# VectorE in the order of emission, column sums that yield to mixing steps, and 16 transposes fewer, in a two-layer hybrid mixer on one core

## The chip, the cores and the metric

The kernel runs on one core of a Trainium2 chip. The metric is the device time of one execution in microseconds (us), as the median of several runs; lower is better.

## What is computed

Two layers, each one pre-norm mixer with adaptive modulation; 256 latent tokens and 256 context tokens of width 2048, all in f32. The reference, cut to what matters:

```python
proj = h @ w_in                      # h: modulated RMSNorm of the tokens
q, k, v = heads(proj...)             # 8 heads of 128; q and k with 2-D rope (latent tokens)
y_f = (fourier_mix(f_x) * silu(f_g)) @ w_up_fourier
y_p = (pool_mix(p_x) * silu(p_g)) @ w_up_pool
o_f, s_f = retention_scan(q, k, v, log_gamma[0], s0_fwd)
o_b, s_b = retention_scan(flip(q), flip(k), flip(v), log_gamma[1], s0_bwd)
y_r = (head_rms(o_f + o_b) * silu(r_g)) @ w_up_ret
g = sigmoid(gate_logits)             # three merge gates of width 2048
out = (g_0 * y_f + g_1 * y_p + g_2 * y_r) @ w_out
x = x + gate * out                   # gate, shift, scale come from silu(c) @ w_ada
```

Only the latent tokens come out. In the last layer the context tokens are therefore needed for the retention state alone (their k and v).

## The kernel before

**Weights as a stream.** Every large product is made of three products in a rounded f32 format: hi·hi, lo·hi and hi·lo, where a value is split into a rounded part (hi) and its remainder (lo). `mm3` (L149) issues the three on TensorE (L151 to L153). The weights pass as *chunks* of two k-tiles (128 rows each) by up to 512 columns; some 520 of them, here numbered from 0. `stream` (L243) goes through them; in iteration i it

- prepares chunk i+2: ScalarE writes `whi` (L206), VectorE subtracts to get `wlo` (L207), three buffers each;
- starts the load of chunk i+4 on SyncE's queue (L196, `raw`, four buffers);
- issues the products of chunk i, 24 matmuls of 128x512 where there are four token tiles or column groups ("four units"), 12 where there are two;
- may run one *background unit* (below).

**Mixing steps.** What lies between the large products (rope, head transposes, retention states, scores, head norms, Fourier and pooling steps, splits) is put into a queue as small steps (`Steps`, `mix.append(fn, gap, after)`). After each unit of a chunk, `products` calls `mix.passed(us)`, which issues the steps that are due: `after` is the time in us from its entry, `gap` the time until the next step may follow. So a step's matmuls get their place between the units' matmuls when the program is built. The steps that matter here: `rope_a` (two GpSimd products, L597, per tile), `rope_b` (VectorE, L604 and L605), `heads_T` (four TensorE transposes per head, L684, and a ScalarE copy, L686), `decayed` (L692), `decays_a` (L708, L709), `scores` (L732, L734), `norm_b` (a VectorE reciprocal L766 and a product L767), `gated` (product L614, then a split of the result: hi on ScalarE L431, lo on VectorE L432).

**Background units.** The modulation needs silu(c) @ w_ada for the second layer, computed as column sums on VectorE: 512 KB of w_ada are loaded (`bgraw`, two buffers), then four scalar_tensor_tensor on 128x512 follow (L468; the first of a sum is L466), or two for units of one vector. They are queued in `bg`.

**What sets the order.** TensorE runs in the order in which the program emits its instructions, from the first streamed block to the end: the whole kernel is under `manual_schedule` with TensorE alone. VectorE, ScalarE, GpSimd and SyncE run in an order of the framework's scheduler, which places each engine's instructions by its own estimate of when their inputs are ready.

**Chunk numbers used below** (layer 0, four units, about 5.45 us each): K of head half 0: 0 to 7, Q: 8 to 15, V, K and Q of half 1: 16 to 39, retention gates to 55, merge gates and up-projections from 56 to 215, output projection 216 to 255 (from 240 on two units). Last layer: q 256 to 263, v, k, q, v, k to 303, retention gates 304 to 319, merge gates and up-projections 320 to 479, output projection to the end (mostly two units, 2.72 us). The mixing of a block runs while the next ones stream. At the end of the output projection the residual is added (L1011, L1012), ScalarE sums squares (L1017) and takes a root (L1021), VectorE reduces and inverts (L1020, L1022) and prepares a row scale (L1077).

```python
        for i in range(n):
            prepare(i + 2)
            ahead(i + 4)
            chunks[i][0].products(chunks[i][1], parts.pop(i))
            if i > 5 and i % 8 in (1, 3, 5, 6, 7) and bg:
                bg.popleft()()
```

Of the kernel before, what the change touches and what calls it, by code (L numbers as in the profile page):

```python
# [19 lines left out]
P = 128  # L20
# [4 lines left out]
SEQ = 256  # L25
# [18 lines left out]
def hybrid_kernel(ctx: ExitStack, tc: tile.TileContext, a: dict, out: bass.AP):  # L44
# [15 lines left out]
    def acc():  # L60
        return accp.tile([P, 512], F32, tag="acc", name=nm("acc"))

    def mx():
        return mxp.tile([P, 512], F32, tag="mx", name=nm("mx"))
# [95 lines left out]
    bg = deque()  # L160
# [21 lines left out]
    mix = Steps()  # L182
# [58 lines left out]
    def stream(blocks):  # L241
        chunks = [(b, k0) for b in blocks for k0 in range(0, b.nkt, 2)]
        n = len(chunks)  # L243
        raws, parts = {}, {}

        def ahead(i):
            if i < n:
                raws[i] = chunks[i][0].load(chunks[i][1])

        def prepare(i):  # L250
            if i < n:
                parts[i] = chunks[i][0].split(chunks[i][1], raws.pop(i))

        for i in range(4):
            ahead(i)
        for i in range(2):
            prepare(i)
        yield
        for i in range(n):
            prepare(i + 2)  # L260
            ahead(i + 4)
            chunks[i][0].products(chunks[i][1], parts.pop(i))
            if i > 5 and i % 8 in (1, 3, 5, 6, 7) and bg:
                bg.popleft()()


# [1 line left out]
    with tc.tile_pool(name="start", bufs=1) as sp:  # L268
# [128 lines left out]
        v0_acc = [acc() for _ in range(4)]  # L397
        rg_acc = [acc(), mx(), mx()]
# [126 lines left out]
    def layer(l):  # L525
        last = l == DEPTH - 1
        tok0, ntok = (0, NTOK) if not last else (SEQ, SEQ)
        seqs = (0, 1) if not last else (1,)
        tiles = (0, 1, 2, 3) if not last else (2, 3)
# [45 lines left out]
        def evac(ps):  # L575
            o = g()
            S.copy(o, ps)  # L577
            return o
# [11 lines left out]
        def rope_a(src, t):  # L590
            rope4 = cst["rope"].rearrange("p (t k c) -> p t k c", t=2, k=2)
            o, r2 = src[t], g()
            pv = o.rearrange("p (h f x c) -> p h f x c", h=4, f=2, x=2)
            rv = r2.rearrange("p (h f x c) -> p h f x c", h=4, f=2, x=2)
            sv = rope4[:, t - 2, 1, :].rearrange("p (f x c) -> p f x c", f=2, x=2)
            for x in range(2):
                G.tensor_tensor(rv[:, :, :, x, :], pv[:, :, :, 1 - x, :], sv[:, :, x, :].unsqueeze(1).to_broadcast([P, 4, 2, 32]), op=ALU.mult)  # L597
            rope_r[t] = r2

        def rope_b(src, t):  # L600
            rope4 = cst["rope"].rearrange("p (t k c) -> p t k c", t=2, k=2)
            o = src[t]
            ov = o.rearrange("p (h c) -> p h c", h=4)
            V.tensor_tensor(ov, ov, rope4[:, t - 2, 0, :].unsqueeze(1).to_broadcast([P, 4, P]), op=ALU.mult)  # L604
            V.tensor_tensor(o, o, rope_r.pop(t), op=ALU.add)  # L605
# [16 lines left out]
        class Half:  # L622
# [11 lines left out]
            def k_done(self, t, ps):  # L634
                self.k[t] = evac(ps)
                if t == 3:
                    for t2 in (2, 3):
                        mix.append(lambda t2=t2: rope_a(self.k, t2), gap=0.8, after=2.0)
                    mix.append(lambda: self.decayed(0), gap=1.6)
                    for t2 in (2, 3):  # L640
                        mix.append(lambda t2=t2: rope_b(self.k, t2), gap=1.0)
                    mix.append(lambda: (self.state(0), self.decayed(1)), gap=1.6)
                    for hh in range(4):
                        mix.append(lambda hh=hh: self.heads_T(self.k, (0, 1, 2, 3), self.kT, hh))
                    mix.append(lambda: self.state(1))
                    if last:
                        self.queue_heads()

            def q_done(self, t, ps):
                self.q[t] = evac(ps)  # L650
                if t == 3:
                    for t2 in (2, 3):
                        mix.append(lambda t2=t2: rope_a(self.q, t2), gap=1.2, after=2.0)
                    for t2 in (2, 3):
                        mix.append(lambda t2=t2: rope_b(self.q, t2), gap=1.0)
                    for hh in range(4):
                        mix.append(lambda hh=hh: self.heads_T(self.q, tiles, self.qT, hh))
                    if not last:
                        self.queue_heads()
# [65 lines left out]
            def scores(self, hh):  # L725
                E = self.dec[hh][0]
                for s in seqs:
                    ps = mx()
                    qs = self.qT[hh][:, s * SEQ - tok0:s * SEQ - tok0 + SEQ]
                    for jt in range(2):  # L730
                        k0 = s * SEQ + jt * P
                        T.matmul(ps[:, jt * SEQ:(jt + 1) * SEQ], self.kT[hh][:, k0:k0 + P], qs, start=True, stop=True)  # L732
                    self.at[hh, s] = g()
                    V.scalar_tensor_tensor(self.at[hh, s], ps, QSCALE, E, op0=ALU.mult, op1=ALU.mult)  # L734
# [295 lines left out]
        if last:  # L1030
# [7 lines left out]
            def done(j, t, ps, c0=0, n=512):  # L1038
                xo = projected(j, t, ps, c0, n)
                V.tensor_tensor(xo, xo, fgs[j][:, c0:c0 + n], op=ALU.mult)  # L1040
                xg.setdefault(t, []).append((xo, 512 * j + c0, n))
                if 512 * j + c0 + n == D:
                    for i, (xo, o, n) in enumerate(xg[t]):
                        if i % 2:
                            S.activation(xo, xo, AF.Copy, scale=rs[t])
                        else:
                            V.tensor_scalar(xo, xo, rs[t], None, op0=ALU.mult)
                        nc.sync.dma_start(out=out[0, (t - 2) * P:(t - 1) * P, o:o + n], in_=xo)
# [7 lines left out]
            for c0 in (0, 256):  # L1056
                blocks.append(Block(wview("w_out", l, 512 * 3, 512), KT, 512, [("T", c0, 3 * P - tok0, 256)], flat(m),
                                    lambda u, ps, c0=c0: done(3, 3, ps, c0, 256), keep=kept))
# [67 lines left out]
    blocks0, halves0, rg_done0 = layer(0)  # L1126
    blocks1, _, _ = layer(1)
    for j in range(4):
        bg_mod(1, j)
    run = stream(blocks0 + blocks1)  # L1130
    next(run)
    for t in range(4):
        halves0[0].v_done(t, v0_acc[t])
    for i, ps in enumerate(rg_acc):
        rg_done0(i, ps)
    for _ in run:
        pass


def _constants():  # L1140
# [78 lines left out]
```

## Time and profile before

| what | value |
|---|---|
| median of 3 runs | 2446.63 us (2446.52 to 2446.91) |
| the profiled execution | 2445.55 us, its span 2443.8 us |
| mean granted TensorE clock | 0.995 |
| TensorE busy | 2392.4 us (98%) |
| VectorE / ScalarE / GpSimd busy | 1320.6 (54%) / 870.4 (36%) / 240.3 us (10%) |

The table says that TensorE is busy nearly all of the span; 100% minus its share is what any change of order can win without removing matmuls. Durations of single instructions and places of waits are not in it; they are in the rows further down. Two things help in reading those. A listed matmul lasts 0.39 us, but the next one starts 0.227 us later, because matmuls overlap; the step between starts is the cost. Instructions on VectorE start up to about 0.08 us before the listed end of the one before.

### The profile page before, as it was taken

The page shows a single profiled execution, that of the slowest core. Times are in us where ns is not written, and L with a number is a line of the kernel's source. Part 1 is how long each engine was busy: PE and PEld are TensorE (multiplying, and loading weights), DVE is VectorE, ACT ScalarE, POOL GpSimd, SP SyncE. Part 2 cuts the span into 40 slices and gives each one's busy share as a digit, 9 for nine tenths or more (in the row PEclk, how much of TensorE's full clock was granted, in tenths as well). Part 3 has the DMA queues.
Part 4 walks back from the last instruction along what each step waited for, and adds up shares of the span by engine and source line. Part 5 has one row for each costly group of instructions (what it writes and reads, how often), then busy time and mean ns, then how long its engine had stood idle before and what let it go on. Part 6 is the DMA issues. An engine that isn't in the chain of part 4 may idle for free.

```text
span 2443.8 us, 28705 instructions
## 1 busy us (share of the span) xinstructions
PE 2392.4 (98%) x11288; PEld 1967.8 (81%) x11288; DVE 1320.6 (54%) x1656; ACT 870.4 (36%) x1180; POOL 240.3 (10%) x246
## 2 busy tenths in 40 slices
PE   6999999999999999999999999999999999999998
PEld 3678788778888888888888888878889888888886
DVE  4437657768256258644457432653527544545555
ACT  5222332342222232222222322563426444444444
POOL 0000200200000001110011210230302000110100
PEclk9999999999999999999999999999999999999999
DMA  9955424346345336545466343443335666676664
GB/s 338 348 170 173 138 78 148 92 136 213 115 144 187 93 119 210 156 128 169 130 202 215 112 129 112 147 150 103 100 90 146 211 191 180 181 216 183 189 204 146
DMA packets 226471, 396.58 MB, mean 162 GB/s; under 512 B 14032, under 2 KB 55376, under 8 KB 226336
## 3 DMA queue, kind: packets, MB, share of 16 engines
q1 hardware_dynamic: 221088, 379.74, 50.8%
q0 software_dynamic: 5248, 15.01, 2.1%
q8 instruction: 88, 1.44, 0.2%
q14 instruction: 47, 0.39, 0.1%
HBM read 392.60 MB, written 2.10 MB: 162 GB/s over the span
## 4 chain that ended last, share of the span: by engine, by line
PE 81%; issue 8%; DMA 5%; DVE 4%; POOL 1%; ACT 1%; SPq 0%; DVEq 0%; POOLq 0%; ACTq 0%
PE acc L151 25%; PE acc L152 25%; PE acc L153 25%; DVE bga L468 2%; DMA wa<-in_w_ada_dram 2%; DMA bgraw<-in_w_ada_dram 1%; DVE wlo L207 1%; PE mx L323 1%; PE mx L744 1%; PE mx L732 1%; PE mx L747 1%; POOL g L1085 1%; PE mx L701 0%; DMA raw<-in_w_out_dram 0%; PE mx L889 0%
## 5 line engine op out<-in xcount | busy, mean ns | idle before, releaser
L207 DVE TENSOR_TENSOR wlo<-raw,whi 128x1024 fp32r<-128x1024 f32 (+1 forms) x504 | 624.6, 1240 | 824.5 <-ACT whi L206 824.0
L206 ACT ACTIVATE whi<-raw 128x1024 fp32r<-128x1024 f32 (+1 forms) x504 | 529.2, 1050 | 1153.4 <-PE acc L153 553.5
L151 PE MATMUL acc<-whi,hm 128*128 128x512 f32 x1568 | 621.9, 397 | 0.7 <-ACT g L577 0.7
L152 PE MATMUL acc<-wlo,hm 128*128 128x512 f32 x1568 | 611.7, 390 | 2.2 <-DVE wlo L207 2.2
L153 PE MATMUL acc<-whi,hm 128*128 128x512 f32 x1568 | 611.7, 390 | 0.0
L151 PE MATMUL acc<-hm,whi 128*128 128x512 f32 (+1 forms) x1232 | 461.1, 374 | 0.7 <-ACT whi L206 0.7
L153 PE MATMUL acc<-hm,wlo 128*128 128x512 f32 (+1 forms) x1232 | 453.0, 368 | 1.0 <-DVE wlo L207 1.0
L152 PE MATMUL acc<-hm,whi 128*128 128x512 f32 (+1 forms) x1232 | 452.7, 367 | 0.0
L152 PEld LDWEIGHTS acc<-wlo,hm 128*128 128x128 f32 x1568 | 295.1, 188 | 62.7 <-DVE wlo L207 4.1
L153 PEld LDWEIGHTS acc<-whi,hm 128*128 128x128 f32 x1568 | 294.7, 188 | 62.3
L151 PEld LDWEIGHTS acc<-whi,hm 128*128 128x128 f32 x1568 | 295.0, 188 | 61.2 <-ACT g L577 1.1
L468 DVE SCALAR_TENSOR_TENSOR bga<-bgraw,sc,bga 128x512 f32<-128x512 f32 x420 | 311.8, 789 | 53.1 <-DMA bgraw<-in_w_ada_dram 51.5
L151 PEld LDWEIGHTS acc<-hm,whi 128*128 128x128 f32 x1232 | 232.6, 189 | 42.4 <-ACT whi L206 2.2
L153 PEld LDWEIGHTS acc<-hm,wlo 128*128 128x128 f32 x1232 | 232.4, 189 | 40.5 <-DVE wlo L207 2.2
L152 PEld LDWEIGHTS acc<-hm,whi 128*128 128x128 f32 x1232 | 232.6, 189 | 39.4 <-issue 1.4
L852 POOL TENSOR_TENSOR g<-g,g 128x512 f32<-128x512 f32 x32 | 52.7, 1673 | 726.5 <-DVE g L848 726.5
L151 PE MATMUL acc<-g,whi 128*128 128x512 f32 x256 | 99.7, 390 | 0.0
L152 PE MATMUL acc<-g,whi 128*128 128x512 f32 x256 | 99.6, 389 | 0.0
L153 PE MATMUL acc<-g,wlo 128*128 128x512 f32 x256 | 99.6, 389 | 0.0
L597 POOL TENSOR_TENSOR g<-g,g 128x256 f32<-128x256 f32 x32 | 29.6, 954 | 332.4 <-ACT g L577 332.4
L151 PEld LDWEIGHTS acc<-g,whi 128*128 128x128 f32 x256 | 48.1, 188 | 10.1
L152 PEld LDWEIGHTS acc<-g,whi 128*128 128x128 f32 x256 | 48.1, 188 | 10.0
(213 smaller groups left out, 1888.4 us busy)
## 6 DMA issues: line engine op xcount, KB each, us to landing
raw<-in_w_in_dram SPq DMA_DIRECT2D x368, 512.0 KB, 3.7
bgraw<-in_w_ada_dram SPq DMA_DIRECT2D x128, 512.0 KB, 4.3
raw<-in_w_out_dram SPq DMA_DIRECT2D x72, 512.0 KB, 3.6
wa<-in_w_ada_dram SPq DMA_DIRECT2D x128, 256.0 KB, 6.0
raw<-in_w_up_ret_dram SPq DMA_DIRECT2D x32, 512.0 KB, 3.8
raw<-in_w_up_fourier_dram SPq DMA_DIRECT2D x16, 512.0 KB, 3.7
raw<-in_w_up_pool_dram SPq DMA_DIRECT2D x16, 512.0 KB, 4.4
w<-in_w_in_dram SPq DMA_DIRECT2D x8, 512.0 KB, 6.6
```

What stands on the lines that cost most here:

```text
L151: T.matmul(ps, ah, bh, start=first, stop=False)
L152: T.matmul(ps, ah, bl, start=False, stop=False)
L153: at["product"] = T.matmul(ps, al, bh, start=False, stop=last)
L206: S.activation(hi[:, :, 0:w], raw[:, :, 0:w], AF.Copy)
L207: V.tensor_tensor(lo[:, :, 0:w], raw[:, :, 0:w], hi[:, :, 0:w].bitcast(F32), op=ALU.subtract)
L323: T.matmul(ps[32 * g4:32 * g4 + 32, 0:2 * n * P], sc32[:, kt, :], wa[gi, kt // rows][:, kt % rows, :, :].rearrange("p i c -> p (i c)"), st ...
L468: V.scalar_tensor_tensor(accs[ci, v], raw[:, kk, :], s, accs[ci, v], op0=ALU.mult, op1=ALU.add)
L597: G.tensor_tensor(rv[:, :, :, x, :], pv[:, :, :, 1 - x, :], sv[:, :, x, :].unsqueeze(1).to_broadcast([P, 4, 2, 32]), op=ALU.mult)
L732: T.matmul(ps[:, jt * SEQ:(jt + 1) * SEQ], self.kT[hh][:, k0:k0 + P], qs, start=True, stop=True)
L744: T.matmul(o, self.v[2 * s + jt][:, c], at[:, jt * SEQ:(jt + 1) * SEQ], start=jt == 0, stop=jt == 1 and s == 0)
L747: T.matmul(o, self.st[d][:, c], qd[:, d * SEQ:(d + 1) * SEQ], start=False, stop=d == 1)
L852: G.tensor_tensor(merged[d][:, 0:ntok], merged[d][:, 0:ntok], o[:, 0:ntok], op=ALU.add)
```

## The change

Four edits:

1. From the first streamed block on, VectorE too runs in the order of emission (`manual_schedule` with VectorE around the stream). TensorE did so already; the other engines stay with the scheduler.
2. A background unit is run when fewer than two mixing steps are queued and the chunk's number is no multiple of four, instead of at five fixed chunks of eight.
3. Between the rope steps lies more time: `gap` 0.8 to 1.6 for k, 1.2 to 2.5 for q.
4. In the last layer only the latent tokens' keys are transposed: two transposes per head instead of four (eight heads, so 16 fewer), and `scores` counts its columns from there.

```diff
@@ stream @@
-            if i > 5 and i % 8 in (1, 3, 5, 6, 7) and bg:
+            if i > 5 and len(mix.q) < 2 and i % 4 and bg:
                 bg.popleft()()
@@ Half.k_done @@
-                        mix.append(lambda t2=t2: rope_a(self.k, t2), gap=0.8, after=2.0)
+                        mix.append(lambda t2=t2: rope_a(self.k, t2), gap=1.6, after=2.0)
...
-                        mix.append(lambda hh=hh: self.heads_T(self.k, (0, 1, 2, 3), self.kT, hh))
+                        mix.append(lambda hh=hh: self.heads_T(self.k, tiles, self.kT, hh))
@@ Half.q_done @@
-                        mix.append(lambda t2=t2: rope_a(self.q, t2), gap=1.2, after=2.0)
+                        mix.append(lambda t2=t2: rope_a(self.q, t2), gap=2.5, after=2.0)
@@ scores @@
-                        k0 = s * SEQ + jt * P
+                        k0 = s * SEQ - tok0 + jt * P
@@ end of the program @@
     run = stream(blocks0 + blocks1)
-    next(run)
-    for t in range(4):
-        halves0[0].v_done(t, v0_acc[t])
-    for i, ps in enumerate(rg_acc):
-        rg_done0(i, ps)
-    for _ in run:
-        pass
+    with tc.manual_schedule(engines={mybir.EngineType.DVE}):
+        next(run)
+        for t in range(4):
+            halves0[0].v_done(t, v0_acc[t])
+        for i, ps in enumerate(rg_acc):
+            rg_done0(i, ps)
+        for _ in run:
+            pass
```

`tiles` is (0, 1, 2, 3) in layer 0 and (2, 3) in the last; `tok0` is 0 and 256.

What the order becomes on VectorE is seen in three places. A row gives the line, the operation, and output<-inputs with numbers that differ between the two programs; `bga` is a column sum, `wlo` a chunk's remainder.

**The rope of q, half 0** (chunks 15 to 18). Before, the last of the column sums ahead of it, then the rope:

```order
L468 SCALAR_TENSOR_TENSOR bga_2208<-bgraw_2455,sc,bga_2208 128x512
L468 SCALAR_TENSOR_TENSOR bga_2206<-bgraw_2543,sc,bga_2206 128x512
L468 SCALAR_TENSOR_TENSOR bga_2208<-bgraw_2543,sc,bga_2208 128x512
L604 TENSOR_TENSOR g_1983<-g_1983,g_1379 128x512
L604 TENSOR_TENSOR g_1991<-g_1991,g_1379 128x512
L207 TENSOR_TENSOR wlo_2000<-raw_1923,whi_1999 128x1024
L605 TENSOR_TENSOR g_1983<-g_1983,g_2012 128x512
L605 TENSOR_TENSOR g_1991<-g_1991,g_2022 128x512
```

Now:

```order
L207 TENSOR_TENSOR wlo_1952<-raw_1883,whi_1951 128x1024
L207 TENSOR_TENSOR wlo_1990<-raw_1919,whi_1989 128x1024
L207 TENSOR_TENSOR wlo_2030<-raw_1955,whi_2029 128x1024
L604 TENSOR_TENSOR g_1979<-g_1979,g_1381 128x512
L605 TENSOR_TENSOR g_1979<-g_1979,g_2002 128x512
L604 TENSOR_TENSOR g_1987<-g_1987,g_1381 128x512
L605 TENSOR_TENSOR g_1987<-g_1987,g_2019 128x512
L207 TENSOR_TENSOR wlo_2078<-raw_1993,whi_2077 128x1024
```

The six column sums that stood right ahead of the rope are gone from here; the four rope instructions stand together behind the `wlo` of chunk 19.

**The head norms of half 1** (chunks 55 to 61). Before, one reciprocal between two `wlo` at most:

```order
L766 RECIPROCAL g_3421<-g_3421 128x512
L207 TENSOR_TENSOR wlo_3635<-raw_3603,whi_3634 128x2x128
L207 TENSOR_TENSOR wlo_3651<-raw_3620,whi_3650 128x2x128
L207 TENSOR_TENSOR wlo_3673<-raw_3638,whi_3672 128x2x128
L767 TENSOR_TENSOR g_3420<-g_3420,g_3421 128x512
L766 RECIPROCAL g_3459<-g_3459 128x512
L207 TENSOR_TENSOR wlo_3685<-raw_3654,whi_3684 128x2x128
L207 TENSOR_TENSOR wlo_3707<-raw_3676,whi_3706 128x1024
L767 TENSOR_TENSOR g_3458<-g_3458,g_3459 128x512
L207 TENSOR_TENSOR wlo_3727<-raw_3688,whi_3726 128x1024
```

Now, from the `wlo` of chunk 58 on:

```order
L207 TENSOR_TENSOR wlo_3614<-raw_3587,whi_3613 128x1024
L766 RECIPROCAL g_3346<-g_3346 128x512
L767 TENSOR_TENSOR g_3345<-g_3345,g_3346 128x512
L766 RECIPROCAL g_3390<-g_3390 128x512
L767 TENSOR_TENSOR g_3389<-g_3389,g_3390 128x512
L766 RECIPROCAL g_3447<-g_3447 128x512
L767 TENSOR_TENSOR g_3446<-g_3446,g_3447 128x512
L207 TENSOR_TENSOR wlo_3654<-raw_3603,whi_3653 128x1024
L766 RECIPROCAL g_3486<-g_3486 128x512
L767 TENSOR_TENSOR g_3485<-g_3485,g_3486 128x512
L614 TENSOR_TENSOR g_2406<-g_2406,g_3437 128x512
L432 TENSOR_TENSOR g_3687<-g_2406,g_3686 128x512
```

Three reciprocals with their products now stand between two `wlo`; behind them come pairs of a gate product (L614) and its split (L432), and four column sums before the `wlo` of chunk 61.

**The start of the output projection of layer 0** (chunk 216). The 16 splits of the merged branches, which its products read, stood one or two per `wlo`, from that of chunk 208 to that of chunk 218, before:

```order
L207 TENSOR_TENSOR wlo_9313<-raw_9244,whi_9312 128x1024
L432 TENSOR_TENSOR hm_9643<-g_4013,hm_9642 128x512
L207 TENSOR_TENSOR wlo_9347<-raw_9278,whi_9346 128x1024
L432 TENSOR_TENSOR hm_9647<-g_4021,hm_9646 128x512
L432 TENSOR_TENSOR hm_9651<-g_4029,hm_9650 128x512
L207 TENSOR_TENSOR wlo_9377<-raw_9316,whi_9376 128x1024
```

Now all 16 follow the `wlo` of chunk 218:

```order
L848 TENSOR_TENSOR g_9564<-acc_9593,g_9564 128x512
L207 TENSOR_TENSOR wlo_9639<-raw_9570,whi_9638 128x1024
L432 TENSOR_TENSOR hm_9645<-g_3896,hm_9644 128x512
L432 TENSOR_TENSOR hm_9649<-g_3904,hm_9648 128x512
L432 TENSOR_TENSOR hm_9653<-g_3912,hm_9652 128x512
L432 TENSOR_TENSOR hm_9657<-g_3920,hm_9656 128x512
```

The first ones have moved from eight chunks ahead of their use to the moment of it. In the same way the instructions at the end of the output projection (L1011 to L1022) now stand in one piece per tile between two `wlo`, and the last layer's reciprocals stand two and four together. The column sums of the second layer's output gates, which were done in layer 0 before, now come in the last layer's merge-gate blocks.

## Rows read from the trace of the kernel before

**Rows 1.** Profile page, section 1: busy time of each engine.
```profile
PE 2392.4 (98%) x11288; PEld 1967.8 (81%) x11288; DVE 1320.6 (54%) x1656; ACT 870.4 (36%) x1180; POOL 240.3 (10%) x246
```

**Rows 2.** Waits of TensorE: line <- releaser: us, times, longest.
```profile
PE mx L732 <- DVE g L734: 5.9, 1, 5.9
PE mx L684 <- DVE g L605: 5.0, 3, 4.6
```

**Rows 3.** Stretches: length, busy PE, PEld, DVE, ACT, POOL, granted clock, DMA.
```profile
250.00:262.00 12.00, 7.32 (x31) 5.64 (x30) 12.00 (x17) 1.81 (x3) 2.10 (x2) 0.82 0.62 181
262.00:275.00 13.00, 13.00 (x60) 10.61 (x59) 11.36 (x18) 6.04 (x10) 1.06 (x1) 0.91 0.68 219
440.00:456.00 16.00, 10.10 (x38) 8.02 (x37) 16.00 (x19) 5.39 (x10) 10.63 (x10) 0.79 0.24 64
465.00:530.00 65.00, 63.25 (x277) 51.39 (x276) 38.75 (x43) 27.23 (x40) 5.17 (x6) 1.00 0.39 122
530.00:1560.00 1030.00, 1029.11 (x4597) 848.29 (x4596) 538.22 (x653) 280.57 (x341) 70.30 (x65) 1.00 0.49 150
1560.00:1630.00 70.00, 67.03 (x302) 53.86 (x301) 54.08 (x77) 54.34 (x105) 36.41 (x40) 1.00 0.52 161
```

**Rows 4.** Stretches behind the two longest waits, and one near the end, same columns.
```profile
260.00:262.00 2.00, 1.72 (x5) 1.23 (x6) 2.00 (x5) 0.59 (x1) 0.00 (x0) 0.50 0.65 162
...
452.00:454.00 2.00, 2.00 (x5) 1.63 (x6) 2.00 (x4) 0.00 (x0) 0.00 (x0) 0.50 0.23 66
454.00:456.00 2.00, 2.00 (x7) 1.52 (x7) 2.00 (x4) 0.00 (x1) 0.00 (x0) 0.60 0.32 29
...
2410.00:2416.00 6.00, 4.13 (x18) 2.77 (x16) 4.34 (x8) 2.35 (x6) 0.00 (x0) 1.00 0.09 13
```

**Rows 5.** VectorE's timeline at the rope of q: start, us, instruction.
```profile
251.43 1.75 DVE L207 TENSOR_TENSOR wlo<-raw,whi 128x1024 fp32r<-128x1024 f32 x1
253.11 4.05 DVE L468 SCALAR_TENSOR_TENSOR bga<-bgraw,sc,bga 128x512 f32<-128x512 f32 x6
...
259.42 1.28 DVE L605 TENSOR_TENSOR g<-g,g 128x512 f32<-128x512 f32 x2
```

**Rows 6.** TensorE's timeline: four transposes and the next matmul; a wait near the end.
```profile
265.39 0.60 PE L684 MATMUL mx<-ident,g 128*128 128x128 f32 x4
265.75 0.48 PE L151 MATMUL acc<-whi,hm 128*128 128x512 f32 x1
...
2413.61 0.50 PE L152 MATMUL acc<-g,hm 128*128 128x512 f32 x1 [1.72 <-DVE g L213]
```

**Rows 7.** ScalarE's and VectorE's timelines: the two splits of one chunk (two units).
```profile
2384.50 1.06 ACT L206 ACTIVATE whi<-raw 128x1024 fp32r<-128x1024 f32 x1 [1.66 <-PE acc L153]
...
2385.60 1.23 DVE L207 TENSOR_TENSOR wlo<-raw,whi 128x1024 fp32r<-128x1024 f32 x1 [1.49 <-ACT whi L206]
```

**Rows 8.** Groups of VectorE instructions by line and shape: busy, mean ns | idle before.
```profile
L207 DVE TENSOR_TENSOR wlo<-raw,whi 128x1024 fp32r<-128x1024 f32 x496 | 621.5, 1253 | 817.7 <-ACT whi L206 817.2
L468 DVE SCALAR_TENSOR_TENSOR bga<-bgraw,sc,bga 128x512 f32<-128x512 f32 x420 | 311.8, 789 | 53.1 <-DMA bgraw<-in_w_ada_dram 51.5
...
L766 DVE RECIPROCAL g<-g 128x512 f32<-128x512 f32 x8 | 26.6, 3342 | 1.9 <-ACT g L762 1.9
...
L432 DVE TENSOR_TENSOR g<-g,g 128x512 fp32r<-128x512 f32 x24 | 17.2, 720 | 11.0 <-ACT g L431 10.9
...
L766 DVE RECIPROCAL g<-g 128x256 f32<-128x256 f32 x8 | 13.7, 1733 | 0.6 <-ACT g L762 0.6
...
L767 DVE TENSOR_TENSOR g<-g,g 128x512 f32<-128x512 f32 x8 | 5.4, 682 | 0.0
...
L767 DVE TENSOR_TENSOR g<-g,g 128x256 f32<-128x256 f32 x8 | 3.1, 400 | 0.0
```

**Rows 9.** VectorE's timeline at an end of the output projection, same columns.
```profile
1565.92 0.16 DVE L1022 RECIPROCAL rs<-rs 128x1 f32<-128x1 f32 x1 [0.38 <-ACT rs L1021]
```

**Rows 10.** Profile page, section 5: GpSimd's rope products.
```profile
L597 POOL TENSOR_TENSOR g<-g,g 128x256 f32<-128x256 f32 x32 | 29.6, 954 | 332.4 <-ACT g L577 332.4
```

## The prediction

> **What bounds the kernel now.** I read the profile in this order: shares of the engines, waits of TensorE, then the stretches around those waits. TensorE is busy 98% of the span and VectorE 54% [rows 1], so a change of VectorE's order can only win where TensorE waits for VectorE. The list of waits names two long ones: 5.9 us for a score (L734) and, of 5.0 us, one of 4.6 for the rope of q (L605) [rows 2]. The stretches tell how rare that is: from 530 to 1560 us TensorE is idle for 0.9 of 1030 us [rows 3]. What there is to win lies in four stretches [rows 3]: 12.00 − 7.32 = 4.7 us idle at 250 to 262, 16.00 − 10.10 = 5.9 at 440 to 456, 65 − 63.25 = 1.75 at 465 to 530 and 70 − 67.03 = 3.0 at 1560 to 1630; 15.3 in all.
>
> The two long ones cost more than their idle time. Behind each, TensorE runs at a granted clock of 0.50, its lower level, 1.2 GHz [rows 4]. At half clock half the time is lost: 0.9 in 260 to 262 [rows 4] and 13 × (1 − 0.91) = 1.2 in 262 to 275 [rows 3]; 1.0 and 0.8 in 452 to 456 [rows 4]. That is 3.8 us.
>
> **What the change takes away.** VectorE's timeline shows the cause at the rope of q: it is never idle, and six column sums (4.05 us) run ahead of the rope, which ends at 259.42 + 1.28 = 260.7 [rows 5], after TensorE has stood still for over 4 us. In the new order these sums are gone from there, and at the scores too. At 465 to 530 a reciprocal delays a `wlo`, and at 1560 to 1630 sums of squares, splits and rope collide; the old waits there end with the old order, and what the new one puts in their place is counted below. Gain: 15.3 + 3.8 = 19.1 us.
>
> Transposes: four take 265.75 − 265.39 = 0.36 us of TensorE's time [rows 6], so 16 take 1.4. They lie between matmuls on the bounding engine, so all of it counts. Their ScalarE copies get shorter; ScalarE is busy 36% and its copies hide behind matmuls, so nothing for that. Gain in all: **20.5 us**.
>
> **What the order of emission adds.** Now each `wlo` waits for everything emitted ahead of it, also for VectorE instructions that themselves wait for ScalarE. First the slack. ScalarE's split of chunk i+2 starts when chunk i does (a buffer comes free) and takes 1.06; `wlo` starts 1.10 behind it and takes 1.23 [rows 7], so it is ready 2.3 us into chunk i. TensorE needs it 0.23 us (one matmul) into chunk i+2, two chunks later: a reserve of 8.8 us with chunks of 5.45, of 3.4 with chunks of 2.72. Where VectorE has less extra work than that, the order costs nothing; I count the places where it has more. Neighbours on VectorE overlap by about 0.07 us (251.43 + 1.75 against 253.11 [rows 5]), which I take off.
>
> *Four hard ones,* in which only VectorE's own durations or a plain dependency enter:
> - Start of the output projection: 16 splits (0.72 each [rows 8]) stand behind the `wlo` of chunk 218, which isn't there before 2.3 us into chunk 216; the first is ready at 2.3 + 0.7 = 3.0, needed at 0.23. **2.8 us.** Before, they ran ahead in time that nobody waited for (the stretch from 530 [rows 3]).
> - Reciprocals of half 1: between the `wlo` of chunk 58 and that of 61 stand four reciprocals of 3.34 and four products of 0.68 (16.1), five gate products of 0.68 (3.4), four splits of 0.72 that each wait some 0.46 (10.9 / 24) for ScalarE (4.7), four sums of 0.79 (3.2) and three `wlo` of 1.25 (3.8) [rows 8]: 31.2, less 20 × 0.07 = 29.8. There is time from 2.3 us into chunk 56 to 0.23 into chunk 61, 5 × 5.45 − 2.1 = 25.2. **4.5 us**, where before 1.75 were lost.
> - Reciprocals of the last layer, half the width but with chunks of 2.72: four × (1.73 + 0.40), eight products and eight splits of 0.40 [rows 8], seven waits of some 0.5, six `wlo` of 1.25: 25.9, less 26 × 0.07 = 24.1. The time is 8 × 2.72 + 0.23 − 2.3 = 19.7. **4.4 us**; before there was no wait.
> - Rope of the last q: four reciprocals and products (8.5) now stand behind the `wlo` of chunk 293 and ahead of the rope. Two `wlo` and four rope instructions of 0.64 (1.28 for two [rows 5]) later, 2.3 + 8.5 + 2.5 + 2.6, less 10 × 0.07 = 15.2 us into chunk 291, the last one is done; its transposes stand 6 matmuls into chunk 293, at 2 × 5.45 + 1.4 = 12.3. **2.9 us.**
>
> Sum 14.6.
>
> *Soft ones,* which rest on how ScalarE's order, still the scheduler's, falls:
> - The ends of the output projection: residual, squares, reduce, root, inverse, twice in a row between two `wlo`, with VectorE waiting for ScalarE inside (0.38 us for a root even where other work filled part of the time [rows 9]). I estimate some 8 us of this per end against 5.7 to the next need (two chunks and 0.23): 2.0 to 2.8 at two ends, and 1.5 for a row scale behind a `wlo` that is not ready before 2.3 us: 6.3.
> - Two smaller ends in the last layer, 0.75 each; the kernel's tail, where splits stand behind both tiles' residual, 0.9; the first half's reciprocals, 0.9; the rope of both q of layer 0, four instructions behind the `wlo` of chunk 19 (2.3 + 2.4 = 4.7 us into chunk 17, transposes after 18 matmuls, 4.1), 0.55 each.
>
> Sum 10.7 if all come in full, 0 if ScalarE's order fills the gaps. Nothing in the trace decides between these ends, so I take half, 5.4.
>
> *Clock.* The waits of 4.7 and 5.9 us were followed by half clock, at 1.9 us each (3.8 / 2). One of 1.72 us near the end [rows 6] was not: the clock stays at 1.00 from 2410 to 2416 [rows 4]. The hard waits lie between, so I take one loss, 1.9, with 0 and 7.6 as ends.
>
> *Column sums.* The other half of the sums' move costs nothing: in the blocks of merge gates VectorE does one `wlo` (1.25) and up to four sums (3.2) in a chunk of 5.45; in the last layer, one `wlo` and two sums (1.6) in 2.72. The loads go with them, on SyncE's queue behind `raw`; a late load there would show as a wait for DMA, up to 3 us as I judge from the tightness, taken as 0.
>
> **Sum.** 14.6 + 5.4 + 1.9 − 20.5 = +1.4 us on the profiled execution's 2445.55; the median of the runs is 1.1 us above that, 2446.63, so **2448 us**. Measurement can tell about 0.2%, 4.9 us, from no change; this isn't.
>
> The row of a `wlo` beside GpSimd's rope products shows 1.75 us instead of about 1.23 [rows 5, 7]: 0.5 more. The Trainium skill (SBUF — State Buffer, "Who interferes with whom") says more: a VectorE instruction with two inputs in SBUF that meets a GpSimd instruction reading SBUF is blocked for the whole of it. By that rule a `wlo` at each of the three ropes of q would lose up to a whole L597 (0.95 [rows 10]), 2.9 us in all, and the sum would be 2451. The row is the smaller, and I keep to it.
>
> **Rivals.**
> - *Faster: the waits go, the new ones hide.* If VectorE gets ahead where I see it late (the hard waits at half size, 7.3, the soft ones at a quarter, 2.7, no clock loss), the time is 2446.6 + 10.0 − 20.5 = 2436. For it: 1030 us with 0.9 idle show how much reserve the stream has. Against: the four hard places follow from order and durations.
> - *Slower: each new wait takes the clock with it.* At chunks 216, 61, 293 and 320 on, hard and soft waits in full (25.3) and 7.6 of clock: 2446.6 + 32.9 − 20.5 = 2459. It decides from new losses of 25.4 us on. For it: two of two waits over 4 us ended at half clock [rows 4]. Against: all four hard ones are shorter than those two. The Trainium skill (TensorE: Matmul & The Clock Gate, "HAM oscillation") warns of just this, gaps between bursts of matmuls that each bring the slow clock back; the rows agree for the long gaps.
> - *The order hardly changes.* Then only the transposes are saved: 2445. The rows of order speak against it.
>
> **How the numbers follow.** No measurable change 0.38 (my sum 0.35, unchanged order 0.03), faster 0.33, slower 0.29. The hard places alone carry 7.3 to 14.6, the soft ones 0 to 10.7, the clock 0 to 7.6: from 2433 to 2459. I leave some off both ends, 2434 to 2457.
>
> **What would show it.** Right: no waits for L605 and L734 over 1 us in layer 0; new waits for L432 at chunk 216 (2.8), for `wlo` at chunk 61 (4.5) and at 320 to 326 (4.4), for L605 at 293 (2.9); idle time of TensorE about as before. Wrong for the faster side: TensorE's busy share near 98.5% with none of these waits over 1.5 us. Wrong for the slower side: clock at 0.50 behind several of them. 96 instead of 112 transposes (L684) in either case.

## The result, and the profile after

The changed kernel takes **2472.6 us** (median of 4 runs, 2469.4 to 2474.1) beside 2446.6 for the kernel before: ratio 1.0105, 95% interval 1.0087 to 1.0122. That is 26 us slower, and 15.6 us above the end of the stated range. Three executions of some 3400 us, at a granted clock of about 0.66 (two of the run e4_transposes below, one of the kernel before beside it), are left out of all ratios and intervals.

The profiled execution spans 2471.0 us, 27.2 more than before. Section 1 of its page, to set beside [rows 1]:

```profile
PE 2400.7 (97%) x11272; PEld 1972.5 (80%) x11272; DVE 1319.4 (53%) x1656; ACT 873.1 (35%) x1182; POOL 235.6 (10%) x246
```

TensorE has 16 instructions fewer and is busy 8.3 us longer (2400.7 − 2392.4); the other 18.9 us of the 27.2 are idle time. Busy time that grows with fewer instructions means slower instructions, so the clock is the first suspect. The waits of TensorE in the changed kernel from 200 us on, as in [rows 2]:

```profile
PE acc L152 <- DVE wlo L207: 13.0, 10, 5.3
PE mx L486 <- ACT g L431: 4.5, 1, 4.5
PE acc L153 <- DVE wlo L207: 4.4, 2, 3.6
PE mx L684 <- DVE g L605: 4.1, 4, 2.1
PE acc L152 <- DVE g L213: 3.9, 1, 3.9
PE acc L153 <- DVE hm L432: 3.5, 1, 3.5
PE mx L744 <- DVE g L734: 2.5, 2, 1.5
```

The two long waits of before are gone: none is left for L732, and of the four for L605 two of 1.1 us together are in layer 0 and two of 3.0 at the last rope of q, a new place. In their place stand 12 waits for `wlo`, the remainder of a streamed weight, one for a split of the merged branches (L432), and one for ScalarE (L431). Where they lie, with the columns of [rows 3]:

```profile
250.00:275.00 25.00, 24.34 (x116) 19.98 (x115) 12.99 (x14) 10.48 (x16) 4.71 (x6) 1.00 0.29 85
...
500.00:520.00 20.00, 15.62 (x61) 12.16 (x60) 17.59 (x23) 6.11 (x8) 2.05 (x3) 0.91 0.45 134
1390.00:1405.00 15.00, 11.48 (x44) 8.98 (x43) 11.16 (x16) 8.61 (x15) 7.18 (x8) 0.89 0.42 139
1555.00:1575.00 20.00, 17.32 (x80) 13.58 (x80) 10.39 (x17) 12.79 (x23) 4.97 (x6) 1.00 0.41 136
1580.00:1602.00 22.00, 16.34 (x62) 12.62 (x62) 16.51 (x26) 14.08 (x31) 8.56 (x10) 0.84 0.61 189
...
1765.00:1785.00 20.00, 16.98 (x67) 13.26 (x66) 9.70 (x11) 3.50 (x6) 0.00 (x0) 0.83 0.20 54
...
1900.00:1922.00 22.00, 18.13 (x76) 13.66 (x76) 18.14 (x28) 9.92 (x15) 3.11 (x5) 1.00 0.61 175
2105.00:2125.00 20.00, 14.90 (x53) 11.41 (x52) 10.33 (x17) 8.20 (x13) 0.69 (x1) 0.83 0.34 101
...
2430.00:2450.00 20.00, 16.08 (x65) 12.80 (x64) 12.40 (x20) 8.14 (x16) 0.00 (x0) 0.91 0.39 130
```

Length minus busy PE is the idle time of a stretch; the clock is the third column from the end. The rope of q (250 to 275) has 0.7 us left. The second row is the reciprocals of half 1 (4.4 us), then the start of the output projection (3.5), its two ends (2.7 and 5.7), the last rope of q (3.0), the last layer's reciprocals (3.9), a gate of the last layer (5.1) and the tail (3.9). In six of these the clock column is below 1. Two stretches of 2 us behind the waits show its level:

```profile
1594.00:1596.00 2.00, 2.00 (x6) 1.57 (x5) 2.00 (x5) 1.41 (x4) 0.00 (x0) 0.50 0.61 171
...
2118.00:2120.00 2.00, 2.00 (x6) 1.56 (x5) 0.00 (x0) 0.00 (x0) 0.00 (x0) 0.50 0.08 26
```

What half clock cost can be summed from the trace: busy time times (1 − clock), over stretches of 1 us, gives 1.6, 1.7, 2.5, 2.9, 3.0 and 1.7 us at the six places, 13.3 in all, and 4.0 at the two places of the kernel before.

Three places in detail. VectorE's timeline behind the reciprocals of half 1:

```profile
504.71 0.69 DVE L432 TENSOR_TENSOR g<-g,g 128x512 fp32r<-128x512 f32 x1 [0.70 <-ACT g L431]
...
512.62 2.73 DVE L468 SCALAR_TENSOR_TENSOR bga<-bgraw,sc,bga 128x512 f32<-128x512 f32 x4
515.27 1.22 DVE L207 TENSOR_TENSOR wlo<-raw,whi 128x1024 fp32r<-128x1024 f32 x1
```

VectorE is late by its own work, and the `wlo` that TensorE waits for stands behind four column sums that nobody needs yet. In the order of emission it can't pass them, nor use the 0.70 us in which it waits for ScalarE.

VectorE's timeline at the second end of the output projection:

```profile
1581.63 1.84 DVE L432 TENSOR_TENSOR hm<-g,hm 128x256 fp32r<-128x256 f32 x2
1583.39 1.75 DVE L207 TENSOR_TENSOR wlo<-raw,whi 128x1024 fp32r<-128x1024 f32 x1
...
1587.78 0.16 DVE L1020 TENSOR_REDUCE rs<-sst 128x1 f32<-128x4 f32 x1 [0.79 <-ACT g L1017]
1588.45 0.16 DVE L1022 RECIPROCAL rs<-rs 128x1 f32<-128x1 f32 x1 [0.52 <-ACT rs L1021]
...
1592.19 1.22 DVE L207 TENSOR_TENSOR wlo<-raw,whi 128x1024 fp32r<-128x1024 f32 x1
```

From the `wlo` at 1583.39 to the next one 8.8 us pass, with a chunk of 2.72. And VectorE comes to this end without a reserve: beside GpSimd's products (L1085) the `wlo` ahead takes 1.75 us, not 1.22, and two splits take 1.84.

```profile
1577.15 9.29 POOL L1085 TENSOR_TENSOR g<-g,g 128x256 f32<-128x256 f32 x8
```

The Trainium skill (SBUF — State Buffer, "Who interferes with whom") says that a VectorE instruction with two inputs in SBUF contends with a GpSimd instruction that reads SBUF; the trace agrees that it is slowed, by 0.53 us here.

ScalarE's timeline at the gate of the last layer:

```profile
2109.93 0.42 ACT L431 ACTIVATE g<-g 128x256 fp32r<-128x256 f32 x1 [1.48 <-DVE g L912]
2110.36 1.28 ACT L815 ACT_TABLE_LOAD   x1
2111.66 1.08 ACT L815 ACTIVATE g<-acc 128x512 f32<-128x512 f32 x2
2112.63 1.06 ACT L206 ACTIVATE whi<-raw 128x1024 fp32r<-128x1024 f32 x1
2113.57 0.63 ACT L431 ACTIVATE g<-bga 128x512 fp32r<-128x512 f32 x1
```

TensorE's order has the sum of the last gate (L486) at this place, and the sum needs the split (L431) that ends this list. ScalarE, in the scheduler's order, does a table load, two activations and a chunk's split first.

### The profile page after: what moved, and what is told of

Same layout as the page of the kernel before. It is cut to its first block, busy times and chain, and to the rows that moved or that the text cites. A ratio compares the mean times of both kernels' runs of the same rounds, so it can differ in the third digit from the quotient of the medians.

```text
span 2471.0 us, 28724 instructions
## 1 busy us (share of the span) xinstructions
PE 2400.7 (97%) x11272; PEld 1972.5 (80%) x11272; DVE 1319.4 (53%) x1656; ACT 873.1 (35%) x1182; POOL 235.6 (10%) x246
## 5 line engine op out<-in xcount | busy, mean ns | idle before, releaser
L468 DVE SCALAR_TENSOR_TENSOR bga<-bgraw,sc,bga 128x512 f32<-128x512 f32 x420 | 298.7, 763 | 4.3 <-DMA bgraw<-in_w_ada_dram 3.1
L852 POOL TENSOR_TENSOR g<-g,g 128x512 f32<-128x512 f32 x32 | 43.6, 1394 | 727.9 <-DVE g L848 727.9
L432 DVE TENSOR_TENSOR g<-g,g 128x512 fp32r<-128x512 f32 (+1 forms) x48 | 30.0, 624 | 59.8 <-ACT g L431 59.8
L151 PEld LDWEIGHTS acc<-g,whi 128*128 128x128 f32 x256 | 48.1, 188 | 10.1
```

The lines of the kernel that those rows point to most:

```text
L151: T.matmul(ps, ah, bh, start=first, stop=False)
L432: V.tensor_tensor(hl[:, 0:n], src[:, 0:n], hh[:, 0:n].bitcast(F32), op=ALU.subtract)
L468: V.scalar_tensor_tensor(accs[ci, v], raw[:, kk, :], s, accs[ci, v], op0=ALU.mult, op1=ALU.add)
L852: G.tensor_tensor(merged[d][:, 0:ntok], merged[d][:, 0:ntok], o[:, 0:ntok], op=ALU.add)
```

## The experiments

**Theory O:** the order of emission makes the new waits, each at its own place: what is emitted late or in a block comes late, and `wlo` behind it. **Theory S:** the moved column sums make the loss. The first four runs part the change. Before, on their chip: 2447.4 us.

**e1_order_only.** The kernel before with VectorE's order alone.

```diff
     run = stream(blocks0 + blocks1)
-    next(run)
...
+    with tc.manual_schedule(engines={mybir.EngineType.DVE}):
+        next(run)
...
```

> Only VectorE's order of emission is added to the kernel before (old rule for column sums, old rope gaps, all transposes). Theory O (the order itself makes the new waits: start of the output projection, reciprocals, ends, last rope): the same waits come, and column sums stand among rope and scores as well, so 2472 us or more. Theory S (the moved column sums make the loss): about 2447 us, within 5.

Measured 2497.0 us (2496.0 to 2498.8), ratio 1.0207 (1.0191 to 1.0223): 50 us slower. Theory S is out; the order alone costs more than the whole change. Its waits of TensorE come at L732 too, where VectorE's timeline has four column sums and a `wlo` ahead of the scores (445.08 to 450.52), and are longer at L684:

```profile
PE acc L152 <- DVE wlo L207: 18.2, 12, 5.3
PE acc L153 <- DVE wlo L207: 10.1, 5, 5.7
PE mx L684 <- DVE g L605: 5.6, 5, 2.3
...
PE mx L732 <- DVE g L734: 4.3, 2, 2.4
```

**e2_no_order.** The changed kernel without that block.

```diff
-    with tc.manual_schedule(engines={mybir.EngineType.DVE}):
-        next(run)
...
+    next(run)
...
```

> The changed kernel without VectorE's order of emission (new rule for sums, new gaps, 16 transposes fewer stay). Theory O: the new waits go and the old waits at the rope of q and at the scores go too, since the sums stay away from them: about 2430 us (2446.6 less most of 20.5). Theory S: the loss stays, 2465 us or more, and TensorE again waits 4 to 6 us for L431 at a gate sum in the last layer.

Measured 2435.7 us (2434.2 to 2436.3), ratio 0.9954 (0.9939 to 0.9970): 11.7 us faster than before and 37 faster than the change. So the other three edits are worth having, and the order loses all of it and more. The gain is 6 us short of the expectation: the rope's wait is halved, not gone, and the gate wait of the last layer is there in the scheduler's order too.

```profile
PE mx L486 <- ACT g L431: 2.9, 1, 2.9
PE mx L684 <- DVE g L605: 2.6, 2, 2.3
```

**e3_old_sums.** The changed kernel with the old rule for column sums.

```diff
-            if i > 5 and len(mix.q) < 2 and i % 4 and bg:
+            if i > 5 and i % 8 in (1, 3, 5, 6, 7) and bg:
```

> The changed kernel with the old rule for the column sums (five of eight chunks). Theory O: the order's waits stay, some grow because sums stand among rope and reciprocals, and only the gate wait in the last layer (8.5 us with its clock loss) goes: 2463 to 2475 us. Theory S: 2447 to 2452 us.

Measured 2481.7 us (2479.7 to 2484.9), ratio 1.0148 (1.0130 to 1.0166). Within the order of emission the new rule is worth 9 us; that is outside the ranges of both theories, and more than I gave it. The gate wait (L486) is gone, as expected.

**e4_transposes.** Edit 4 alone.

```diff
-                        mix.append(lambda hh=hh: self.heads_T(self.k, (0, 1, 2, 3), self.kT, hh))
+                        mix.append(lambda hh=hh: self.heads_T(self.k, tiles, self.kT, hh))
...
-                        k0 = s * SEQ + jt * P
+                        k0 = s * SEQ - tok0 + jt * P
```

> Only the 16 transposes are taken out of the kernel before. All theories: 1.4 us less, 2445.2 us; a scheduler that shifts other work could make it differ by a few us either way.

Measured 2442.8 us at the median, ratio 0.9982 (0.9972 to 0.9992): by the ratio 4.4 us less, with an interval from 2 to 7. The sign is clear; that it is more than 1.4 isn't explained. The waits for L732 (5.6) and L605 (5.2) are the old ones.

The next runs price single places. Before, on their chip: 2445.5 us.

**e5_out_ahead.** Twelve of the 16 splits are emitted two per chunk in the last merge-gate block, when TensorE has read the buffers that they take.

```diff
+                during = {k0: lambda k0=k0: (split_merged(k0 - 2), split_merged(k0 - 1)) for k0 in range(2, 14, 2)}
-                fblock(C_MG + b * D + 512 * j, 4, gate_done)
+                fblock(C_MG + b * D + 512 * j, 4, gate_done, during if final and j == 3 else None)
...
-                for d in range(KT):
+                for d in sorted(merged):
                     split_merged(d)
```

> The changed kernel, but 12 of the 16 splits of the merged branches are emitted two per chunk ahead of the output projection, as soon as their buffers come free. Theory O (place in the order is the price): the wait of 3.7 us for the first split at chunk 216 goes, with the 1.3 us of half clock behind it; 2472.6 - 5 = 2467.6 us. Rival (the wait is for ScalarE's half of the split or for the buffers, not for VectorE's queue): within 1.5 us of 2472.6.

Measured 2465.1 us (2462.8 to 2467.7), ratio 1.0079 (1.0064 to 1.0094): 7.5 less than the change (6.4 by the ratios, since before reads 1.1 us less on this chip). The wait (3.5) and the half clock behind it (1.7) make 5.2 of that. The stretch around chunk 216 has no idle time left:

```profile
1385.00:1405.00 20.00, 20.00 (x90) 16.57 (x89) 9.98 (x11) 6.53 (x8) 10.23 (x12) 1.00 0.58 173
```

In the profiled execution a further gain comes from a place that this edit doesn't touch. At the last rope of q TensorE waits as in the change (below, the second of its two waits), but the clock stays at 1.00, where the change lost 2.9 us:

```profile
1768.93 0.33 PE L684 MATMUL mx<-ident,g 128*128 128x128 f32 x1 [2.13 <-DVE g L605]
...
1760.00:1785.00 25.00, 22.00 (x100) 17.70 (x99) 11.19 (x12) 6.32 (x10) 0.00 (x0) 1.00 0.28 83
```

**e6_spread_norms.** One reciprocal per chunk.

```diff
                 for hh in range(4):
-                    mix.append(lambda hh=hh: self.norm_b(hh))
+                    mix.append(lambda hh=hh: self.norm_b(hh), gap=4.2 if last else 6.0)
```

> The changed kernel with one reciprocal of the head norms per chunk instead of two to four between two wlo. Theory O: the waits behind reciprocals go (1.4 us at half 0, 5.1 at half 1, 4.5 in the last layer): 2472.6 - 11.0 = 2461.6 us. Rival (gate products and splits, each waiting for ScalarE inside VectorE's order, are what is late): the waits move a few chunks on, and less than 4 us are gained.

Measured 2459.9 us (2459.7 to 2461.0), ratio 1.0058 (1.0043 to 1.0073): 12.7 less than the change (11.5 by the ratios). The stretches of the norms of layer 0 and of the last layer in this run, 0.4 and 1.1 us idle:

```profile
335.00:530.00 195.00, 194.57 (x893) 162.11 (x892) 114.29 (x123) 73.06 (x101) 25.55 (x27) 1.00 0.34 101
1895.00:1922.00 27.00, 25.89 (x113) 20.82 (x112) 20.06 (x29) 14.61 (x20) 3.10 (x5) 1.00 0.75 235
```

**e7_sums_sooner.** e2 with column sums in every chunk with few steps queued.

```diff
-            if i > 5 and len(mix.q) < 2 and i % 4 and bg:
+            if i > 5 and len(mix.q) < 2 and bg:
```

> Without VectorE's order of emission (2435.7 us so far), and column sums in every chunk with fewer than two steps queued, not in three of four. If the gate wait in the last layer comes of where the last sum falls among the pooling steps, it goes with its clock loss: 2435.7 - 6 = 2430 us. Rival: the sums come nearer to rope and scores again, and a wait of some us there takes it back: 2433 to 2440 us.

Measured 2436.0 us (2434.6 to 2436.3), ratio 0.9958 (0.9941 to 0.9974): no gain over e2, as the rival had it, though not where it said. The gate wait is gone, and TensorE waits for `wlo` in the middle of layer 0 instead:

```profile
1105.00:1130.00 25.00, 20.26 (x80) 15.58 (x79) 18.57 (x24) 5.97 (x8) 0.00 (x0) 0.93 0.72 238
```

**e8_order_to_24.** VectorE's order for chunks 0 to 23 only, by a second `yield` in `stream`.

```diff
+            if i == 24:
+                yield
             prepare(i + 2)
...
-        for _ in run:
-            pass
+        next(run)
+    for _ in run:
+        pass
```

> The changed kernel with VectorE in the order of emission for chunks 0 to 23 only, scheduled after that. The 3.3 us wait at the rope of q that the scheduler's order still has goes, with about 1.6 us of half clock, and none of the later waits of the order comes: 2435.7 - 4 = 2431.7 us. Rival: the order costs from its first chunk on, or the seam between the two costs: 2435 us or more.

Measured 2436.4 us (2436.0 to 2438.6), ratio 0.9965 (0.9952 to 0.9978): nothing gained over e2. TensorE waits 2.9 us at the rope, as there, and a wait of 2.1 us for the scores' scaling (at 287 us) is new. VectorE's timeline at the rope shows why: column sums stand between its steps here too (in this kernel L468, L604 and L605 are L470, L606 and L607).

```profile
257.11 0.73 DVE L470 SCALAR_TENSOR_TENSOR bga<-bgraw,sc,bga 128x512 f32<-128x512 f32 x1
257.77 0.68 DVE L607 TENSOR_TENSOR g<-g,g 128x512 f32<-128x512 f32 x1
258.38 0.67 DVE L606 TENSOR_TENSOR g<-g,g 128x512 f32<-128x512 f32 x1
258.98 0.73 DVE L470 SCALAR_TENSOR_TENSOR bga<-bgraw,sc,bga 128x512 f32<-128x512 f32 x1
```

The likely reading is that sums emitted after the seam (chunk 24, where the order ends) fill VectorE before it; that isn't shown, since it wasn't tried apart.

The last three, before 2444.6 us on their chip:

**e9_late_root.** At the end of layer 0, reduce, root and inverse become a mixing step of their own (`row_root`).

```diff
+                        if j == 3 and c2 == 0:
+                            mix.append(lambda: [row_root(2 * s + t2, 3) for t2 in range(2)], gap=0.0)
```

> The changed kernel, but the row norms' reduce, root and inverse at the end of layer 0 are emitted as a mixing step of their own, some 2 us later, so that VectorE no longer waits for ScalarE's squares and roots between residuals. Theory O with ScalarE inside (the chain through ScalarE is what makes the ends late): the waits at the two ends (0.9 + 0.8 at 1560 to 1563, 0.6 + 5.8 at 1585 to 1594, about 2 of half clock) shrink to 2.5 us or less, 2472.6 - 7 = 2465.6 us. Rival (VectorE is behind before the end begins, since GpSimd's products beside it stretch wlo to 1.75 and the splits to 0.92 us): more than half of the 5.8 stays, 2468 us or more.

Measured 2470.1 us (2468.8 to 2470.8), ratio 1.0104 (1.0090 to 1.0118): 2.4 less than the change, and by the ratios the same as it. The idle time at the second end falls from 5.7 to 3.1 us, at the first from 2.7 to 2.3 (a later row scale takes most of it back):

```profile
1555.00:1575.00 20.00, 17.67 (x85) 14.42 (x84) 11.22 (x18) 13.90 (x25) 6.26 (x8) 1.00 0.47 135
1575.00:1602.00 27.00, 23.93 (x102) 18.68 (x101) 23.16 (x33) 20.76 (x41) 12.77 (x15) 0.94 0.67 212
```

So the chain through ScalarE is about half of the second end, and the rest stays, as the rival had it. In the time even that half hardly shows: the tail's wait is 4.9 us here instead of 3.9, the half clock in the first 200 us cost 5.0 us in this profiled execution and 1.7 in the change's, and more wasn't found.

**e10_sums_last.** e2, with the sums of the last layer in every free chunk and those of layer 0 as in the change.

```diff
-            if i > 5 and len(mix.q) < 2 and i % 4 and bg:
+            if i > 5 and len(mix.q) < 2 and (i % 4 or i > 300) and bg:
```

> Without VectorE's order of emission, column sums in three of four chunks in layer 0 (new rule) and in every chunk with fewer than two steps queued in the last layer. If place alone makes both waits: the gate wait of the last layer goes (4.5 us and 2 of half clock) as with sums in every chunk, and the wait at 1109 to 1127 us of that run does not come: 2435.7 - 6 = 2430 us. Rival: the gain is eaten elsewhere, 2434 us or more.

Measured **2429.2 us** (2427.5 to 2429.6), ratio 0.9936 (0.9922 to 0.9949): 15.4 us faster than the kernel before and 43 faster than the change (41 by the ratios), the best of the study. The scores and the gate of the last layer wait for nothing; the rope of q still does, 3.0 us:

```profile
440.00:456.00 16.00, 16.00 (x74) 13.57 (x73) 5.48 (x8) 2.06 (x3) 3.63 (x6) 1.00 0.09 26
...
2060.00:2092.00 32.00, 32.00 (x151) 26.79 (x150) 18.18 (x28) 16.63 (x28) 3.53 (x2) 1.00 0.55 162
```

**e11_rope_gap.** e10 with `gap` 4.0 instead of 2.5 after each `rope_a` of q in layer 0.

> As the run before, with a gap of 4.0 instead of 2.5 after each rope_a of q in layer 0, which puts the transposes that wait some 3 us later between the products. The remaining wait at the rope of q (2.5 + 0.8 us and 1.6 of half clock) goes: 2430 - 4 = 2426 us. Rival: the later steps of the same queue become late in turn: no gain.

Measured 2432.5 us (2431.4 to 2433.8), ratio 0.9951 (0.9938 to 0.9963): 3.3 slower than e10. The wait at the rope falls to one of 0.95 us, for a `wlo`, but one of 3.7 us for `wlo` comes at 1097 us:

```profile
1092.34 0.75 DVE L468 SCALAR_TENSOR_TENSOR bga<-bgraw,sc,bga 128x512 f32<-128x512 f32 x1 [6.55 <-DMA bgraw<-in_w_ada_dram]
...
1096.26 1.22 DVE L207 TENSOR_TENSOR wlo<-raw,whi 128x1024 fp32r<-128x1024 f32 x1
```

Here the scheduler's order has sums ahead of a `wlo`, and VectorE waits 6.55 us for their data.

**e12_three_mends.** The order of emission with e5, e6 and e10's rule together; before 2445.6 us on its chip.

> The changed kernel, VectorE still in the order of emission, with three mends at once: splits of the merged branches ahead of the output projection, one reciprocal per chunk, and column sums in every free chunk of the last layer. If the new waits are separate places with separate prices, the gains add up: 7.5 + 12.7 as measured one by one, and about 7.5 for the gate wait with its clock: 2472.6 - 27.7 = 2445 us, about the kernel before. Rival (the places share their reserve, and mending one moves the wait to another, VectorE in this order being too late as a whole): 2455 us or more.

Measured 2455.3 us (2451.2 to 2457.5), ratio 1.0039 (1.0025 to 1.0053): 17 us less than the change (16 by the ratios), 10 short of the sum, at the rival's bound. The three places are mended in the trace; what is left are those that nobody touched, the second end, the last rope and the tail:

```profile
1570.00:1590.00 20.00, 14.31 (x55) 10.92 (x54) 13.63 (x24) 11.73 (x25) 5.33 (x7) 0.83 0.67 194
1755.00:1780.00 25.00, 22.73 (x98) 18.21 (x97) 9.33 (x10) 7.78 (x12) 0.00 (x0) 0.93 0.25 75
2410.00:2430.00 20.00, 14.90 (x54) 11.82 (x54) 11.14 (x19) 6.54 (x14) 0.00 (x0) 0.83 0.29 96
```

The profiled run was the second fastest of its five, at 2451.7. Part of the missing 10 us was probably never there: the profiled execution of e5 kept the clock at the last rope besides, and here that clock falls again (0.93 above). The tail, at 5.1 us idle, is 1.2 longer than in the change. Where the rest went isn't settled.

## Why the prediction was wrong

**What is taken away: right.** The old waits at rope and scores are gone, and e2 shows that the edits without the order give 11.7 us, the time of the faster rival within 0.4 us; but that rival had the new waits hide, and here they aren't made, so the agreement is luck.

**The four hard places: right.** Expected 2.8, 4.5, 4.4 and 2.9, in sum 14.6; idle in the trace 3.5, 4.4, 3.9 and 3.0, in sum 14.8. e5 and e6 confirm three of them by taking them away; the last rope wasn't tried by itself. Durations times counts against the reserve of two chunks is a sound way to size an order.

**The clock: the step that failed most.** I took one loss of 1.9 us, since the hard waits were shorter than the old ones of 4.7 and 5.9. The clock column is below 1 in six stretches. TensorE's busy time grew by 8.3 us though 1.4 us of transposes went, so half clock costs 9.7 more than the 3.8 of before, some 13.5 us (13.3 by the sum over stretches): even above the upper end that I had set, 7.6. The gap between a wait that kept the clock (1.72) and one that lost it (4.7) was wide open, and I filled it in favour of the change; the slower rival named this mechanism, and it came.

**The soft places: halved, but they came in full and more.** The ends were to cost up to 6.3 us and cost 2.7 + 5.7 = 8.4 of idle time. I had counted each end against a full reserve, but VectorE came to the second one with none, after `wlo` of 1.75 us beside GpSimd. I had seen that row [rows 5] and used it at the rope alone. The tail grew too, to 3.9 us of idle time. The rope's leftover (1.1), the first half's reciprocals (1.25) and the two small ends (1.6) came about as sized in full.

**"The column sums cost nothing": wrong at one place.** The last gate's sum now falls among the pooling steps, where ScalarE's order isn't TensorE's: 5.1 us idle and a fall of the clock. I had looked at VectorE's load and at the DMAs there, not at the ScalarE split between the sum and TensorE. e2 has this wait without the order (2.9 us), e3 with the order and the old rule hasn't; e7, e10 and e12, which place the sum elsewhere, haven't either. So it comes with the new rule, not with the order. The loads of the sums were not late: VectorE's idle time put down to `bgraw` fell from 51.5 us [rows 8] to 3.1. Two waits of the attention product for the scores' scaling (L744 for L734, 2.5 us) weren't foreseen either.

Together: about 8 us of idle time at places not foreseen, about 9 by which soft places exceeded the half I took (the tail with 2.2, beyond its 1.7 of before), and about 12 of clock: 29, where the sum missed by 24.6 (2472.6 against 2448). This is a count of places, and the difference isn't placed in full; 1.4 of it is half clock in the first 200 us, 3.1 in the profiled execution before and 1.7 in the one after.

## What to carry to other kernels

Putting an engine into the order of emission makes every emission place a promise: what is emitted in a block, or at the moment of its use, is late by the length of the block, and everything behind it too. Mend the emission (early splits, one long instruction per chunk) before fixing the order, or leave the order to the scheduler and change only what it may choose from, which here gave the best time. When waits are counted on a busy TensorE, price the long ones with half clock behind them (1.6 to 3.0 us each here), and those of about 2 us as a chance of it.

## What the runs showed of the hardware

In the change's trace single waits of TensorE of 3.5 to 5.3 us were followed by half clock at five places. A series of 1.36, 1.40, 0.93 and 0.18 us with matmuls between (1900 to 1922), 3.9 in sum, kept the clock at 1.00. So the same idle time cost more in one piece than in several, and I had not expected it to be lost as often as this.

The last rope of q lies between: 0.88 and 2.13 us with one transpose between them, and the clock of that stretch is 0.83.

```profile
1773.66 0.47 PE L684 MATMUL mx<-ident,g 128*128 128x128 f32 x1 [2.13 <-DVE g L605]
```

The same pair of waits is in e9, where the clock fell as well, and in e3 and e5, where it stayed at 1.00. Over all traces, from 200 us on, 39 of 40 waits of 2.4 us or more were followed by half clock (the one of 3.52 us in e9 was not), and 9 of 15 between 1.9 and 2.4 us. So for waits of about 2 us one trace doesn't tell what the same wait will cost in another kernel.

In the first 200 us, up to the first chunks of the stream, where no edit is aimed, half clock cost 1.7 us in some traces (the change, e10) and 5.0 in others (e2, e9). So a difference of about 3 us between two profiled executions can come from there alone.
